# Stick-breaking norms for two pairs of heads at once, scaled later, with filling products from the first head on

## The chip, the cores and the metric

The kernel runs on one core of a Trainium2 chip. The metric is the device time of one execution in microseconds (us); lower is better. Five engines work side by side, each through a queue of its own in order: TensorE (PE, matrix products and transposes; its weight loads are shown apart as PEld), VectorE (DVE), ScalarE (ACT), GpSimd (POOL), and SyncE (SP), which issues the DMAs. They wait for each other by semaphores. Tiles live in SBUF, TensorE's results in the banks of PSUM.

## The reference

A residual stream of 512 tokens by 1024 passes two layers of FFN, hybrid mixer, cross attention and FFN, and then two layers of a second block. The change is about the stick-breaking heads of the mixer and what follows them. There are 8 heads of width 64. For each head, with z = q.k/8 and a strictly causal mask:

```
log_beta    = log_sigmoid(z)
log_1m_beta = where(causal, log_beta - z, 0)
between     = reverse_cumsum(log_1m_beta) - log_1m_beta
a           = where(causal, exp(log_beta + between), 0)
sb          = rms_norm(a @ v, sb_out_norm)        # per head, over its 64 values
h           = h + concat(sb, go) @ w_out          # go: gated-DeltaNet heads
h           = h + cross_attention(rms_norm(h), rms_norm(mem))
```

## The kernel before

Everything is float32, and a product of two float32 matrices is made as three products of rounded parts: each operand is split into a high part (`xh`, `wh`, `mh`, `gh`: a cast on ScalarE) and a low part (`xl`, `wl`, `ml`, `gl`: a subtraction on VectorE). Activations lie feature-major, 128 features by 512 tokens to a tile.

A mixer ends with the stick-breaking stage (`stick`, `heads_in_turn`). Heads run in turn, two to a *pair*, and head `hd` is one ahead of head `hd - 1`. For a head, TensorE makes the scores in three PSUM banks (`psz`, L989, L994), ScalarE two sigmoids of each (`sc`, `sb`; L1059, L1060), VectorE four running products along the keys (*scans*, L1064; 128, 384, 256 and 512 columns), and GpSimd multiplies both (L1065). Then ten transposes (L1011), in three groups of 4, 3 and 3 with a PSUM tile `pst` each, turn these weights; ScalarE, VectorE, ScalarE copy them (L1014). After an odd head, `pair_values` (L1028) multiplies the turned weights of both heads with the values into one bank, `pso`.

`use` then norms the pair: copy (`sacc`) and square (`ssq`) on ScalarE; sums over the 64 rows of each head by four small products (L1075); on VectorE mean and epsilon (`sbs`, L1078) and the reciprocal root as an integer start and three Newton steps, twelve instructions of 8 columns (`rsqrt`, L382 to L388, result `sbr`); on TensorE a broadcast of the factors (L1083); on VectorE the scaling (L1084) and the split into `mh`, `ml` (L394, L395).

To keep TensorE busy between these, `fills` deals out *filling products* in steps of six: first the mixer's output product of the other heads (`psd<-gh,wh` and so on, 512 columns, 16 steps), then the memory keys of the cross attention (`psd<-mem,wh`, 256 columns, 32 steps). `STICK_FILL` says how many steps go out after a head's scores, and at its transposes; what is left is drained at the end. The stage has PSUM banks for 2 fills (`d`), 3 scores (`z`), 2 of tag `t` (transposes, sums, broadcasts) and 1 of values.

The cross attention begins with two products that need no norm: the memory values (`x_v`, 16 steps of 12 products) and the rest of the mixer's output product, which reads `mh` and `ml` (`self.rest`, 16 steps). `XV_STEPS` deals them out in turn, 4 and 4.

The order on each engine is laid down when the program is built: the framework takes the instructions in the order of the code, with the weight loads, casts and subtractions (`wr`, `wh`, `wl`; L266 to L268) moved ahead by a priority, and places each by its own estimate of when it can start. On the chip every engine then takes its queue strictly in that order.

Of the kernel before, what the change touches and what calls it, by code (L numbers as in the profile page):

```python
# [18 lines left out]
P = 128  # L19
D = 1024  # L20
S = 512
# [13 lines left out]
AHEAD_FIRST = 70  # L35
ON_POOL = ()
PBUFS = (2, 2, 2, 2)
STICK_FILL = ((0,),) + ((1, 1, 2),) * 8
PARTS_AFTER = 8
PARTS_AHEAD = 1  # L40
XV_STEPS = (4, 4, 4, 0)
DIL_FILL = ((8,),) + ((4, 2, 2),) * 8
FOX_FILL = ((8,), (4, 2, 2), (1, 1, 1), (1, 1, 0), (0, 1, 1), (0, 1, 1), (0, 1, 1), (0, 1, 1), (0, 0, 1))

# [133 lines left out]
class Builder:  # L178
# [193 lines left out]
        return fill  # L372


    def rsqrt(self, x, out, tag):

        nc = self.nc
        n = x.shape[1]
        t = self.small([P, n], tag + "_t", 2)
        y = self.small([P, n], tag + "_y", 2)  # L380
        hx = self.small([P, n], tag + "_h", 2)
# [51 lines left out]
    def mean_rsqrt(self, m, out, eps=1e-6, n=D):  # L433

        self.nc.vector.tensor_scalar(out=m, in0=m, scalar1=1.0 / n, scalar2=eps, op0=ALU.mult, op1=ALU.add)
        self.rsqrt(m, out, "rs")

    def stats(self, h, width=S, tag="n"):

# [254 lines left out]
    def gdn_project(self, T, l, xh, xl, rc, R):  # L694
# [72 lines left out]

        rn = T([P, 2, H, NT], "rn")
        f3 = lambda x: x.rearrange("p a b c -> p (a b c)")
        self.rsqrt(f3(ss), f3(rn), "rq")  # L770
# [159 lines left out]
    def gdn_norm(self, T, t, state, o):  # L930

        nc = self.nc
        H = 4
        z = state["zt"][t]
        sq = self.xp.tile([P, H, P], F32, name=self.uid("osq"), tag="sq", bufs=1)
        nc.scalar.activation(out=sq, in_=o, func=AF.Square)
        so = self.small([P, H], "so")
        nc.vector.tensor_reduce(out=so, in_=sq, op=ALU.add, axis=AX.X)
        nc.vector.tensor_scalar(out=so, in0=so, scalar1=1.0 / GD, scalar2=1e-6, op0=ALU.mult, op1=ALU.add)
        ro = self.small([P, H], "ro")  # L940
        self.rsqrt(so, ro, "rp")
# [89 lines left out]
    def stick(self, T, l, qp, kp, v, mh, ml, fill):  # L1031
# [20 lines left out]
        def weights(hd):  # L1052
# [13 lines left out]
                    p[t] = bt  # L1066
            return p

        def use(pr, op):
            ot, sq = (self.xp.tile([P, S], F32, name=self.uid("s" + n), tag=n, bufs=1) for n in ("acc", "sq"))  # L1070
            nc.scalar.copy(ot, op)
            nc.scalar.activation(out=sq, in_=op, func=AF.Square)
            ssp = self.ps("t", [P, NT, 2])
            for t in range(NT):
                nc.tensor.matmul(ssp[:, t], sq[:, t * P : (t + 1) * P], self.c("pair"), start=True, stop=True)  # L1075
            f = lambda x: x.rearrange("p a b -> p (a b)")
            ss, ro = self.small([P, NT, 2], "sbs", 2), self.small([P, NT, 2], "sbr", 2)
            nc.vector.tensor_scalar(out=ss, in0=ssp, scalar1=1.0 / 64, scalar2=1e-6, op0=ALU.mult, op1=ALU.add)  # L1078
            self.rsqrt(f(ss), f(ro), "sbq")
            ps = self.ps("t")  # L1080
            for t in range(NT):
                for e in range(2):
                    nc.tensor.matmul(ps[64 * e : 64 * e + 64, t * P : (t + 1) * P], ro[:, t, e : e + 1].to_broadcast([P, 64]), self.c("ident"), start=True, stop=True)  # L1083
            nc.vector.scalar_tensor_tensor(out=ot, in0=ot, scalar=gn[:, pr : pr + 1], in1=ps, op0=ALU.mult, op1=ALU.mult)  # L1084
            self.split(mh[:, pr], ml[:, pr], ot)

        self.heads_in_turn(weights, v, T, use, fill)


    def memory_stats(self, T):  # L1090
# [39 lines left out]
    def xattn(self, h, l):  # L1130
        nc = self.nc
        H, W = XH, MEM
        with self.kvs, self.scope(self.uid("xa")) as xp, self.banks(d=3, n=1, z=2, t=2):
# [6 lines left out]
                self.split(v[0][:, t, c], v[1][:, t, c], ps, self.mem_c[:, t : t + 1])  # L1140

            steps = self.dense_tm_steps("x_v", l, 8, self.memp[:, 0], self.memp[:, 1], use_v, nt=2)
            for n in XV_STEPS:
                for _ in range(4):
                    next(self.rest)
                for _ in range(n):
                    next(steps)
            self.drain(self.rest)
            self.drain(steps)
            xh, xl, rc, R = self.norm(h, self.g("xattn_norm", l))  # L1150
# [65 lines left out]
    def final_and_norm(self, h, gain):  # L1216
# [24 lines left out]
        def factors():  # L1241
            m = self.small([P, 2, NT], "ms2", 1)
            ps = self.ps("n", [P, 2, NT])
            for i, x in enumerate((acc, acc2)):
                for j in range(NT):
                    nc.tensor.matmul(ps[:, i, j : j + 1], x[:, j * P : (j + 1) * P], self.c("one"), start=True, stop=True)
            nc.vector.tensor_scalar(out=m, in0=ps, scalar1=1.0 / D, scalar2=None, op0=ALU.mult)
            nc.vector.tensor_scalar(out=m[:, 0], in0=m[:, 0], scalar1=1e-6, scalar2=None, op0=ALU.add)
            nc.vector.scalar_tensor_tensor(out=m[:, 1], in0=m[:, 0], scalar=1e-6, in1=m[:, 1], op0=ALU.mult, op1=ALU.add)
            flat = lambda x: x.rearrange("p a b -> p (a b)")  # L1250
            self.rsqrt(flat(m), flat(both_r), "rs2")

        R = xt("R")
        self.pending.append(factors)
# [52 lines left out]
    def qk_project_steps(self, T, name, l, xh, xl, rc, fox):  # L1307
# [17 lines left out]
        self.rsqrt(flat(ss), flat(rr), "hq")  # L1325
# [80 lines left out]

    def heads_in_turn(self, weights, v, T, use, fill):

        p, pTs = {}, []
        for hd in range(9):  # L1410
            if hd < 8:
                p[hd] = weights(hd)
            if hd == 0:
                fill(0, 0)
                continue
            last = hd - 1
            pTs.append(self.turned_weights(p.pop(last), T, last % 2, fill=lambda i: fill(hd, i)))
            if last % 2:
                use(last // 2, self.pair_values(pTs, v, last // 2))
                pTs = []  # L1420
        fill(9, 0)

    def fox_decay(self, T, fa, l):

# [17 lines left out]
    def second(self, h, l, pT, after_final=False):  # L1442
        nc = self.nc
        self.turn_bank = "n"
        with self.scope(self.uid("sec")) as sp, ExitStack() as st:
# [37 lines left out]
            for _ in range(PARTS_AFTER):  # L1483
# [5 lines left out]
            self.turn_bank = 't'  # L1489
            dil = self.c("dil")  # L1490
            ob = half("ob")
            self.causal_attention(
                T,
                parts_b,
                v,
                None,
                lambda hd, t: dil[:, 384 - t * P : 512],
                lambda pr, ps: nc.vector.tensor_copy(ob[:, pr], ps),
                self.fills([("fq", qk("s_qa")), ("fv", values("s_va")), ("gb", gate("s_gb")), ("fk", qk("s_ka"))], DIL_FILL, got),
                ready,  # L1500
            )
# [154 lines left out]
```

## Time and profile before

| what | value |
|---|---|
| runs | 3204.21, 3196.81, 3198.81 us |
| median | 3198.81 us |
| profiled execution, its own time | 3195.22 us |
| its span, first to last instruction | 3192.9 us |
| TensorE's mean granted clock in it | 0.994 of 2.4 GHz |
| TensorE busy | 3134.1 us, 98% |
| VectorE busy | 2326.2 us, 73% |
| ScalarE busy | 1451.7 us, 45% |
| GpSimd busy | 133.8 us, 4% |

All rows are of the one profiled execution. The page gives sums over the whole span; a table by windows gives the same for stretches, with the granted clock (1.00 is 2.4 GHz, 0.50 is 1.2 GHz). A list of waits names the instruction that waited and the one that let it go. A timeline gives each instruction's start and length, with like neighbours merged into one row. Matmuls are pipelined: the spacing of their starts is what one costs, not the length in its row.

### The profile page before, as it was taken

The numbers are of one execution on the slowest core, as the hardware profiler recorded it, in microseconds if no ns is written. First come the engines' busy times: TensorE is split into PE (matmuls) and PEld (weight loads), VectorE is DVE, ScalarE is ACT, GpSimd is POOL, SyncE is SP. The second block draws the span as 40 slices with busy tenths as digits, with TensorE's granted clock in tenths as the row PEclk, the third lists the DMA queues.
The fourth block names the chain that finished last, engine by engine and source line by source line (L and its number), as shares of the span: only waits on it lengthen the run. The fifth ranks groups of instructions, "written<-read, shape, count | busy, mean of one in ns | idle before, by whom it ended". The sixth has DMA issues, their size and how long they took to land. (4 is left out here: it accounts for less than half of the span.)

```text
span 3192.9 us, 50423 instructions
## 1 busy us (share of the span) xinstructions
PE 3134.1 (98%) x20520; PEld 2718.9 (85%) x20520; DVE 2326.2 (73%) x3952; ACT 1451.7 (45%) x2291; POOL 133.8 (4%) x182
## 2 busy tenths in 40 slices
PE   8999999989999999999999989999999999999999
PEld 7999877778889998999877868889998987799877
DVE  8887567776588877888657686578886667766675
ACT  5344542544443434334452354453343556445563
POOL 0000002220000000000002040000000000000000
PEclk9999999999999999999999999999999999999999
DMA  4332220323233323333221223133332322223223
GB/s 165 97 118 81 87 73 28 95 71 113 67 125 95 107 76 117 100 103 101 70 86 34 82 65 119 60 125 99 101 95 72 100 80 80 76 90 100 72 73 101
DMA packets 86728, 287.32 MB, mean 90 GB/s; under 512 B 10080, under 2 KB 13408, under 8 KB 86496
## 3 DMA queue, kind: packets, MB, share of 16 engines
q1 hardware_dynamic: 86496, 284.10, 28.7%
q8 instruction: 161, 2.64, 0.3%
q14 instruction: 71, 0.58, 0.1%
HBM read 269.38 MB, written 2.10 MB: 85 GB/s over the span
## 5 line engine op out<-in xcount | busy, mean ns | idle before, releaser
L268 DVE TENSOR_TENSOR wl<-wr,wh 128x1024 fp32r<-128x1024 f32 (+3 forms) x384 | 443.1, 1154 | 211.4 <-ACT wh L267 209.4
L267 ACT CAST wh<-wr 128x1024 fp32r<-128x1024 f32 (+3 forms) x384 | 378.1, 985 | 399.4 <-PE psd L274 285.9
L394 ACT CAST sh<-sr 128x1024 fp32r<-128x1024 f32 x252 | 264.8, 1051 | 503.7 <-PE psd L580 474.4
L274 PE MATMUL psd<-xh,wh 128*128 128x512 f32 x960 | 387.0, 403 | 7.2 <-ACT xh L397 7.2
L274 PE MATMUL psd<-xl,wh 128*128 128x512 f32 x960 | 385.5, 402 | 0.2 <-DVE xl L398 0.2
L274 PE MATMUL psd<-xh,wl 128*128 128x512 f32 x960 | 384.9, 401 | 0.2 <-DVE wl L268 0.2
L580 PE MATMUL psd<-xh,sl 128*128 128x256 f32 x1152 | 322.7, 280 | 5.2 <-DVE sl L395 5.2
L580 PE MATMUL psd<-xh,sh 128*128 128x256 f32 x1152 | 322.5, 280 | 0.0
L580 PE MATMUL psd<-xl,sh 128*128 128x256 f32 x1152 | 321.9, 279 | 0.0
L395 DVE TENSOR_TENSOR sl<-sr,sh 128x1024 fp32r<-128x1024 f32 x252 | 307.3, 1220 | 15.1 <-ACT sh L394 14.2
L274 PE MATMUL psd<-wh,xh 128*128 128x256 f32 (+1 forms) x1024 | 292.1, 286 | 1.0 <-ACT wh L267 0.9
L274 PE MATMUL psd<-wh,xl 128*128 128x256 f32 (+1 forms) x1024 | 289.9, 283 | 1.2 <-DVE xl L398 1.1
L274 PE MATMUL psd<-wl,xh 128*128 128x256 f32 (+1 forms) x1024 | 289.0, 283 | 0.0
L274 PE MATMUL psd<-ah,wh 128*128 128x512 f32 x704 | 278.2, 395 | 0.0
L274 PE MATMUL psd<-al,wh 128*128 128x512 f32 x704 | 278.0, 395 | 0.0
L274 PE MATMUL psd<-ah,wl 128*128 128x512 f32 x704 | 277.0, 394 | 0.0
L274 PEld LDWEIGHTS psd<-xh,wh 128*128 128x128 f32 x960 | 181.2, 189 | 53.9 <-ACT xh L397 7.2
L580 PEld LDWEIGHTS psd<-xh,sl 128*128 128x128 f32 x1152 | 216.9, 188 | 6.8 <-DVE sl L395 6.8
L580 PEld LDWEIGHTS psd<-xh,sh 128*128 128x128 f32 x1152 | 216.8, 188 | 5.3
L580 PEld LDWEIGHTS psd<-xl,sh 128*128 128x128 f32 x1152 | 216.8, 188 | 4.8
L274 PEld LDWEIGHTS psd<-xh,wl 128*128 128x128 f32 x960 | 181.5, 189 | 42.1 <-issue 1.2
L274 PEld LDWEIGHTS psd<-xl,wh 128*128 128x128 f32 x960 | 181.5, 189 | 39.9 <-DVE xl L398 1.0
(452 smaller groups left out, 6999.2 us busy)
## 6 DMA issues: line engine op xcount, KB each, us to landing
sr<-w_ffn_in_dram SPq DMA_DIRECT2D x144, 512.0 KB, 3.9
wr<-w_ffn_out_dram SPq DMA_DIRECT2D x96, 384.0 KB, 4.0
wr<-w_ffn_in_dram SPq DMA_DIRECT2D x32, 512.0 KB, 3.8
wr<-w_mix_gdn_dram SPq DMA_DIRECT2D x24, 512.0 KB, 3.7
B<-B SPq DMA_DIRECT2D x40, 256.0 KB, 3.4
wr<-w_ffn_out_dram SPq DMA_DIRECT2D x16, 512.0 KB, 3.4
wr<-w_mix_qk_dram SPq DMA_DIRECT2D x16, 512.0 KB, 3.8
wr<-w_x_k_dram SPq DMA_DIRECT2D x16, 512.0 KB, 3.7
```

Source lines behind the costliest of these rows:

```text
L267: nc.scalar.copy(hi, raw)
L268: (nc.gpsimd if name in ON_POOL else nc.vector).tensor_sub(lo, raw, hi.bitcast(F32))
L274: mm = lambda a, b, first, last: nc.tensor.matmul(ps, a, b, start=first, stop=last, skip_group_check=flip)
L394: nc.scalar.copy(hi, src)
L395: nc.vector.tensor_tensor(out=lo, in0=src, in1=hi.bitcast(F32), op=ALU.subtract)
L580: nc.tensor.matmul(ps[:, j], w[a][:, k, fs], x[b][:, k], start=start and i == 0, stop=k == 3 and i == 2, skip_group_check=True)
```

## The change

Three things are changed, in both layers alike.

The norm of a pair is cut into functions. `use` makes the copy and the square at once as before (the copy of an even pair goes to tile `R`, of an odd pair to `acc`), and returns what is left as a list: for an even pair the sums alone; for an odd pair the sums with one reciprocal root for both pairs (16 columns), an empty step, the scaling of the even pair, and that of the odd pair. `heads_in_turn` takes one function of the list after each of a head's fills, but for the one in the middle. What the last pair leaves goes to the cross attention, which runs it between steps of the memory values.

`STICK_FILL` deals two steps after the first head's scores and five per head in place of four. `XV_STEPS` now holds, in turn, how many of the left-over functions, of the steps of the values and of the rest of the output product.

All norms of the kernel share one set of scratch tiles (`nr_t`, `nr_y`, `nr_h`) in place of a set for each caller.

```diff
-STICK_FILL = ((0,),) + ((1, 1, 2),) * 8
+STICK_FILL = ((2,),) + ((1, 2, 2),) * 8
-XV_STEPS = (4, 4, 4, 0)
+XV_STEPS = ((1, 4, 0), (3, 4, 12), (0, 4, 4))
...
-        t = self.small([P, n], tag + "_t", 2)
+        t = self.small([P, n], "nr_t", 3)
...
+        held = []
+
         def use(pr, op):
-            ot, sq = (self.xp.tile([P, S], F32, name=self.uid("s" + n), tag=n, bufs=1) for n in ("acc", "sq"))
+
+            ot, sq = (self.xp.tile([P, S], F32, name=self.uid("s" + n), tag=n, bufs=1) for n in (("R", "acc")[pr % 2], "sq"))
             nc.scalar.copy(ot, op)
             nc.scalar.activation(out=sq, in_=op, func=AF.Square)
...
+            if pr % 2 == 0:
+                held.append(self.small([P, 2, NT, 2], "sbs", 2))
+            ss = held[-1]
+
+            def sums():
+                ssp = self.ps("t", [P, NT, 2])
+                for t in range(NT):
+                    nc.tensor.matmul(ssp[:, t], sq[:, t * P : (t + 1) * P], self.c("pair"), start=True, stop=True)
+                nc.vector.tensor_scalar(out=ss[:, pr % 2], in0=ssp, scalar1=1.0 / 64, scalar2=1e-6, op0=ALU.mult, op1=ALU.add)
+
+            def scaled(pr, ot, ro):
+                ps = self.ps("t")
+                for t in range(NT):
+                    for e in range(2):
+                        nc.tensor.matmul(ps[64 * e : 64 * e + 64, t * P : (t + 1) * P], ro[:, pr % 2, t, e : e + 1].to_broadcast([P, 64]), self.c("ident"), start=True, stop=True)
+                nc.vector.scalar_tensor_tensor(out=ot, in0=ot, scalar=gn[:, pr : pr + 1], in1=ps, op0=ALU.mult, op1=ALU.mult)
+                self.split(mh[:, pr], ml[:, pr], ot)
+
+            if pr % 2 == 0:
+                held.append(ot)
+                held.append(ss)
+                return [sums]
+            ro = self.small([P, 2, NT, 2], "sbr", 2)
+            even = held[-2]
+
+            def factors():
+                sums()
+                flat = lambda x: x.rearrange("p c a b -> p (c a b)")
+                self.rsqrt(flat(ss), flat(ro))
+
+            return [factors, lambda: None, lambda: scaled(pr - 1, even, ro), lambda: scaled(pr, ot, ro)]
+
+        self.after = self.heads_in_turn(weights, v, T, use, fill)
...
-            for n in XV_STEPS:
-                for _ in range(4):
-                    next(self.rest)
+
+            for first, n, rest in XV_STEPS:
+                for _ in range(first):
+                    self.after.pop(0)()
                 for _ in range(n):
                     next(steps)
+                for _ in range(rest):
+                    next(self.rest)
...
-        p, pTs = {}, []
+
+
+        p, pTs, later = {}, [], []
+
+        def then(hd, i):
+            fill(hd, i)
+            if later and i != 1:
+                later.pop(0)()
+
...
-            pTs.append(self.turned_weights(p.pop(last), T, last % 2, fill=lambda i: fill(hd, i)))
+            pTs.append(self.turned_weights(p.pop(last), T, last % 2, fill=lambda i: then(hd, i)))
             if last % 2:
-                use(last // 2, self.pair_values(pTs, v, last // 2))
+                later = use(last // 2, self.pair_values(pTs, v, last // 2)) or []
```

How the orders differ is shown at three places of the first layer (the second layer's are alike). First VectorE's queue at the second pair's norm, before. `pst` is read for the sums, `sc` are the next head's scans, `sbr` the factors, `sacc` the pair being scaled.

```order
L1078 TENSOR_SCALAR sbs_6467<-pst_6462 128x8
L382 TENSOR_SCALAR sbq_t_6470<-sbs_6467 128x8
...
L1064 SCALAR_TENSOR_TENSOR sc_1064_6504<-sc_1064_6504,consts 128x128
L383 TENSOR_SCALAR sbq_y_6471<-sbq_t_6470 128x8
L1064 SCALAR_TENSOR_TENSOR sc_1064_6504<-sc_1064_6504,consts 128x384
...
L1064 SCALAR_TENSOR_TENSOR sc_1070_6526<-sc_1070_6526,consts 128x512
...
L388 SCALAR_TENSOR_TENSOR sbr_6468<-sbq_t_6470,sbq_y_6471 128x8
L268 TENSOR_TENSOR wl_6797<-wr_6795,wh_6796 128x1024
L1084 SCALAR_TENSOR_TENSOR sacc_6458<-sacc_6458,gains,pst_6485 128x512
```

And now, at the same pair, where one chain serves two pairs; `memT` frees a bank (`psd`) of the memory keys, `pT` is a copy of turned weights.

```order
L1064 SCALAR_TENSOR_TENSOR sc_1076_6542<-sc_1076_6542,consts 128x256
L1084 TENSOR_SCALAR sbs_6262<-pst_6563 128x8
L382 TENSOR_SCALAR nr_t_6569<-sbs_6262 128x16
...
L1064 SCALAR_TENSOR_TENSOR sc_1079_6552<-sc_1079_6552,consts 128x512
L386 TENSOR_TENSOR nr_t_6569<-nr_y_6570 128x16
L1014 COPY pT_1087_6592<-pst_6591 128x384
L387 TENSOR_TENSOR nr_t_6569<-nr_t_6569,nr_h_6571 128x16
L1146 TENSOR_TENSOR memT_6607<-psd_6395,mem_r 128x256
...
L268 TENSOR_TENSOR wl_6710<-wr_6708,wh_6709 128x1024
...
L388 SCALAR_TENSOR_TENSOR sbr_6522<-nr_t_6569,nr_y_6570 128x16
L1064 SCALAR_TENSOR_TENSOR sc_1099_6650<-sc_1099_6650,consts 128x128
```

The chain now has three scans of one head ahead of it, one scan, a copy, a bank's release, a weight's low part and a split inside, and the next head's scans behind it.

Second, TensorE's queue at the same place, before: sums (`ssq`), fills (24 in all, three rows of them shown), the broadcast of `sbr`, and the transposes of the head.

```order
L1075 MATMUL pst_6462<-consts,ssq_6459 128x2 x4
L989 MATMUL psz_6521<-mh_5970,ml_5971 128x512 x2
...
L274 MATMUL psd_6570<-mem_6536,wh_6572 128x256 x2
L274 MATMUL psd_6570<-mem_6536,wl_6573 128x256
L989 MATMUL psz_6620<-B_1030_6354,ml_5971 128x128
L1083 MATMUL pst_6485<-consts,sbr_6468 64x128 x8
L1011 MATMUL pst_6583<-consts,sb_1033_6368 128x128
```

And now (`psd_6612` is the bank that `memT` of the piece above frees).

```order
L1083 MATMUL pst_6563<-consts,ssq_6519 128x2 x4
L1011 MATMUL pst_6584<-consts,sb_1050_6426 128x128
...
L274 MATMUL psd_6611<-mem_6361,wl_6615 128x256
L1011 MATMUL pst_6625<-consts,sb_1050_6426 128x128
...
L274 MATMUL psd_6612<-mem_6361,wh_6614 128x256 x2
...
L989 MATMUL psz_6643<-B_1047_6412,ml_5971 128x128 x2
...
L1090 MATMUL pst_6683<-consts,sbr_6522 64x128 x8
L1011 MATMUL pst_6695<-consts,sb_1072_6529 128x128
```

Between the sums and the broadcast there now stand ten transposes, 24 fills, the next head's scores and 6 fills; before there were two score products, a mask and 24 fills.

Third, TensorE's queue at the end of the stage, before: the last pair's values, 10 fills, sums, 19 fills, the broadcast, and then the rest of the memory keys.

```order
L1028 MATMUL pso_6901<-pT_1152_6876,v_5480 64x128
...
L1075 MATMUL pst_6914<-consts,ssq_6911 128x2 x4
...
L1083 MATMUL pst_6937<-consts,sbr_6920 64x128 x8
...
L274 MATMUL psd_6950<-mem_6536,wl_6983 128x256
```

And now: 36 fills, the sums, 48 products of the memory values (`psd<-wh,mem`), and the broadcasts of two pairs.

```order
L274 MATMUL psd_6927<-mem_6361,wl_6974 128x256
L1083 MATMUL pst_7021<-consts,ssq_6956 128x2 x4
L274 MATMUL psd_7048<-wh_7043,mem_6361 128x256
...
L1090 MATMUL pst_7107<-consts,sbr_6959 64x128 x8
L1090 MATMUL pst_7119<-consts,sbr_6959 64x128 x8
```

The last two pairs are scaled in the cross attention's stage, behind the first four steps of the memory values; the output product that reads them stands 48 products later.

## Rows read from the trace of the kernel before

**Rows 1.** The page, engines: busy us (share of the span) xinstructions.

```profile
PE 3134.1 (98%) x20520; PEld 2718.9 (85%) x20520; DVE 2326.2 (73%) x3952; ACT 1451.7 (45%) x2291; POOL 133.8 (4%) x182
```

**Rows 2.** Windows: stretch and length, busy us of each engine, PEclk, DMA share, GB/s.

```profile
600.00:720.00 120.00, 105.16 (x701) 86.09 (x700) 90.41 (x157) 65.47 (x121) 35.25 (x32) 0.94 0.26 77
720.00:860.00 140.00, 139.96 (x763) 118.15 (x761) 86.76 (x139) 65.57 (x114) 0.00 (x0) 1.00 0.28 91
1820.00:1940.00 120.00, 104.84 (x689) 85.93 (x688) 89.43 (x154) 64.44 (x119) 35.24 (x32) 0.93 0.25 75
1940.00:2080.00 140.00, 139.97 (x763) 118.20 (x762) 86.20 (x139) 64.93 (x113) 0.00 (x0) 1.00 0.29 91
```

**Rows 3.** TensorE's waits, 605 to 715 us: us in total, times, longest.

```profile
PE pst L1083 <- DVE sbr L388: 10.4, 4, 3.5
PE pst L1011 <- POOL sb L1065: 2.3, 1, 2.3
PE pst L1011 <- DVE pT L1014: 1.2, 1, 1.2
PE psz L989 <- DMA mh<-mh: 0.8, 1, 0.8
```

**Rows 4.** TensorE's waits, 1825 to 1935 us.

```profile
PE pst L1011 <- DVE pT L1014: 1.4, 1, 1.4
```

**Rows 5.** Windows around single waits, columns as in rows 2.

```profile
619.00:625.00 6.00, 5.59 (x26) 4.43 (x27) 5.74 (x7) 2.96 (x6) 6.00 (x6) 0.72 0.00 0
...
670.00:676.00 6.00, 5.03 (x35) 4.17 (x35) 3.57 (x9) 1.98 (x4) 0.29 (x1) 0.72 0.27 87
...
1909.00:1919.00 10.00, 7.67 (x47) 7.10 (x47) 5.75 (x13) 2.22 (x5) 1.09 (x1) 0.66 0.16 54
...
1848.00:1851.00 3.00, 1.57 (x9) 1.31 (x9) 3.00 (x5) 2.58 (x5) 3.00 (x3) 1.00 0.50 130
```

**Rows 6.** TensorE's timeline, second pair: start, length, instruction, [idle before it <-releaser].

```profile
661.76 0.84 PE L989 MATMUL psz<-mh,ml 128*128 128x128 f32 x4
...
664.52 0.48 PE L274 MATMUL psd<-mem,wh 128*128 128x256 f32 x2
...
667.43 0.22 PE L989 MATMUL psz<-B,ml 128*128 128x128 f32 x1
670.97 1.38 PE L1083 MATMUL pst<-consts,sbr 128*64 128x128 f32 x16 [3.33 <-DVE sbr L388]
...
676.94 0.93 PE L1011 MATMUL pst<-consts,sb 128*128 128x128 f32 x7
```

**Rows 7.** VectorE's timeline, 653 to 681 us.

```profile
653.03 3.76 DVE L1064 TENSOR_TENSOR_SCAN sc<-sc,consts 128x128 f32<-128x128 f32 x4
656.71 0.53 DVE L1014 COPY pT<-pst 128x384 f32<-128x384 f32 x1
...
660.46 1.23 DVE L268 TENSOR_TENSOR wl<-wr,wh 128x1024 fp32r<-128x1024 f32 x1 [0.20 <-ACT wh L267]
...
664.10 0.17 DVE L1078 TENSOR_SCALAR sbs<-pst 128x8 f32<-128x8 f32 x1 [2.42 <-PE pst L1075]
...
669.33 0.99 DVE L388 SCALAR_TENSOR_TENSOR sbq_y<-sbq_t,sbq_y 128x8 f32<-128x8 f32 x1
...
670.75 0.17 DVE L388 SCALAR_TENSOR_TENSOR sbr<-sbq_t,sbq_y 128x8 f32<-128x8 f32 x1
...
680.42 0.41 DVE L1125 TENSOR_TENSOR memT<-psd,mem_r 128x256 f32<-128x256 f32 x1
```

**Rows 8.** GpSimd's timeline: the products of heads 4 and 5.

```profile
653.61 4.66 POOL L1065 TENSOR_TENSOR sb<-sb,sc 128x127 f32<-128x127 f32 x4 [9.95 <-DVE sc L1064]
...
669.21 1.09 POOL L1065 TENSOR_TENSOR sb<-sb,sc 128x511 f32<-128x511 f32 x1 [1.33 <-DVE sbq_t L386]
```

**Rows 9.** VectorE by shape: xcount, busy us, mean ns, idle before.

```profile
L388 DVE SCALAR_TENSOR_TENSOR sbr<-sbq_t,sbq_y 128x8 f32<-128x8 f32 x8 | 1.3, 166 | 0.3
L388 DVE SCALAR_TENSOR_TENSOR hrr<-hq_t,hq_y 128x32 f32<-128x32 f32 x8 | 1.5, 190 | 0.2
```

More of the change, by code (lines that the diff above doesn't have):

```diff
@@ L372, in fills, with rsqrt @@
         return fill
-    def rsqrt(self, x, out, tag):
+    def rsqrt(self, x, out):
         nc = self.nc
         n = x.shape[1]
-        t = self.small([P, n], tag + "_t", 2)
-        y = self.small([P, n], tag + "_y", 2)
-        hx = self.small([P, n], tag + "_h", 2)
+        t = self.small([P, n], "nr_t", 3)
+        y = self.small([P, n], "nr_y", 3)
+        hx = self.small([P, n], "nr_h", 3)
         nc.vector.tensor_single_scalar(t.bitcast(I32), x.bitcast(I32), 1, op=ALU.logical_shift_right)
@@ L435, in mean_rsqrt @@
         self.nc.vector.tensor_scalar(out=m, in0=m, scalar1=1.0 / n, scalar2=eps, op0=ALU.mult, op1=ALU.add)
-        self.rsqrt(m, out, "rs")
+        self.rsqrt(m, out)
     def stats(self, h, width=S, tag="n"):
@@ L769, in gdn_project @@
         f3 = lambda x: x.rearrange("p a b c -> p (a b c)")
-        self.rsqrt(f3(ss), f3(rn), "rq")
+        self.rsqrt(f3(ss), f3(rn))
         f, ir = T([P, NT, H], "xa"), T([P, H, NT], "ir")
@@ L940, in gdn_norm @@
         ro = self.small([P, H], "ro")
-        self.rsqrt(so, ro, "rp")
+        self.rsqrt(so, ro)
         nc.gpsimd.tensor_tensor(out=z, in0=o.rearrange("p h c -> p (h c)"), in1=z, op=ALU.mult)
@@ L1067, in weights @@
             return p
+        held = []
         def use(pr, op):
-            ot, sq = (self.xp.tile([P, S], F32, name=self.uid("s" + n), tag=n, bufs=1) for n in ("acc", "sq"))
+            ot, sq = (self.xp.tile([P, S], F32, name=self.uid("s" + n), tag=n, bufs=1) for n in (("R", "acc")[pr % 2], "sq"))
             nc.scalar.copy(ot, op)
             nc.scalar.activation(out=sq, in_=op, func=AF.Square)
-            ssp = self.ps("t", [P, NT, 2])
-            for t in range(NT):
-                nc.tensor.matmul(ssp[:, t], sq[:, t * P : (t + 1) * P], self.c("pair"), start=True, stop=True)
@@ L1076, in use @@
[L1076 to L1083, printed above, removed]
@@ L1084, in use @@
-            nc.vector.scalar_tensor_tensor(out=ot, in0=ot, scalar=gn[:, pr : pr + 1], in1=ps, op0=ALU.mult, op1=ALU.mult)
-            self.split(mh[:, pr], ml[:, pr], ot)
-        self.heads_in_turn(weights, v, T, use, fill)
+            if pr % 2 == 0:
[6 more added lines that the diff above has]
+                nc.vector.tensor_scalar(out=ss[:, pr % 2], in0=ssp, scalar1=1.0 / 64, scalar2=1e-6, op0=ALU.mult, op1=ALU.add)
@@ L1250, in factors @@
             flat = lambda x: x.rearrange("p a b -> p (a b)")
-            self.rsqrt(flat(m), flat(both_r), "rs2")
+            self.rsqrt(flat(m), flat(both_r))
         R = xt("R")
@@ L1324, in qk_project_steps @@
         rr = self.small([P, NT, 8], "hrr", 2)
-        self.rsqrt(flat(ss), flat(rr), "hq")
+        self.rsqrt(flat(ss), flat(rr))
         for t in range(NT):
@@ L1416, in heads_in_turn @@
             last = hd - 1
-            pTs.append(self.turned_weights(p.pop(last), T, last % 2, fill=lambda i: fill(hd, i)))
+            pTs.append(self.turned_weights(p.pop(last), T, last % 2, fill=lambda i: then(hd, i)))
             if last % 2:
-                use(last // 2, self.pair_values(pTs, v, last // 2))
+                later = use(last // 2, self.pair_values(pTs, v, last // 2)) or []
                 pTs = []
         fill(9, 0)
+        return later
     def fox_decay(self, T, fa, l):
@@ L1491, in second, with use_b @@
             ob = half("ob")
+            def use_b(pr, ps):
+                nc.vector.tensor_copy(ob[:, pr], ps)
             self.causal_attention(
@@ L1497, in second @@
                 lambda hd, t: dil[:, 384 - t * P : 512],
-                lambda pr, ps: nc.vector.tensor_copy(ob[:, pr], ps),
+                use_b,
                 self.fills([("fq", qk("s_qa")), ("fv", values("s_va")), ("gb", gate("s_gb")), ("fk", qk("s_ka"))], DIL_FILL, got),
```

## The prediction, written before the changed kernel was run

> **What bounds the kernel now.** I read the page's engine line first: TensorE (PE) is busy for 98% of the span and VectorE (DVE) for 73% [rows 1]. So only TensorE's missing 59 us, and any time at its lower clock, can be won without taking work away. The table by stage came next, with the stick-breaking stages (600 to 720 us and 1820 to 1940 us, one per layer) apart from the cross attention behind each. TensorE is busy for 105.2 and 104.8 of 120 us there, and for 140.0 of 140 us in both cross attentions [rows 2]. Half of all that TensorE misses lies in the two stages that the change touches.
>
> Then TensorE's waits in the two stages. Four waits in each are for `sbr`, the norm's factors that VectorE makes: 10.4 us in each layer, the longest 3.5 us. One is for GpSimd's product (2.3 us), one for VectorE's copy of transposed weights (1.2 and, in the second layer, 1.4 us) [rows 3, 4]; the rest of the second layer's list reads as the first's. Last, the granted clock just after such waits: it falls from 2.4 to 1.2 GHz, and a stretch of 6 us has a mean of 0.72, that is 0.28 x 6 = 1.7 us lost. Each layer has three long waits for `sbr`; five of the six such stretches have 0.72, the sixth, at 1909 us, has 0.66 over 10 us, 3.4 us lost. Two more with 0.72, one in each layer, follow the wait for GpSimd (619 us is the first). After the shorter wait of 1.4 us the clock stays at 1.00 [rows 5].
>
> Why `sbr` is late can be read in the first layer's second norm. TensorE finishes what it has at 667.4 + 0.2 us and waits until 670.97 [rows 6]. VectorE starts the norm at 664.10 and ends it at 670.75 + 0.17, 6.8 us, although its twelve small instructions take 0.17 us each when alone: the next head's four scans stand between them, and one of the twelve took 0.99 us [rows 7]. It ended with GpSimd's product (669.21 + 1.09 = 670.30; 669.33 + 0.99 = 670.32) [rows 7, 8].
>
> **The change, part by part.** *The waits for the factors.* The broadcasts of the factors (L1083 before, L1090 after) move from behind one group of fills to behind two heads' transposes, or, for the last two pairs, into the cross attention's stage. If the new places are covered, 2 x 10.4 = 20.8 us of waits go [rows 3], and 5 x 1.7 + 3.4 = 11.9 us of lost clock [rows 5]. The waits for the copy (1.2 + 1.4) go too: twelve 512-column fills now stand ahead of the third group of transposes. Gross: 35.3 us. The wait for GpSimd with its clock, and 0.8 us for a transfer at the stage's start, stay: nothing in front of them is moved.
>
> *The norm itself.* Two chains per layer in place of four, each 16 wide. An instruction of the chain takes 166 ns at 8 columns and 190 ns at 32 [rows 9], so 16 cost between these, and 24 instructions a layer (4 us at least) leave VectorE. TensorE gains from that only through the waits. Sharing one set of scratch tiles among all norms costs nothing: only VectorE writes and reads them, in order.
>
> *The moved fills.* One more step per head, so 36 products (256 columns) are left at the stage's end in place of 96. Their number is the same, so TensorE's work is unchanged; on their way they fill the place of the old waits. SP's weight loads change their order with them (output projection after four loads for the values). TensorE did not wait in that stage before [rows 2]; two staging tiles still run ahead. I take nothing; the other bound is one wait like today's, 3.5 us a layer.
>
> *Is VectorE in time for the new place?* I walk the first layer from the start of the scores of head 5, 661.76 in the trace; call it 0. TensorE: scores and sums 2.8 (661.76 to 664.52), ten transposes about 1.3 (seven took 0.9), 24 fills 2.9 (664.52 to 667.43) [rows 6]. At about 7.0 it wants the second bank of the memory keys, which VectorE frees with `memT` in the middle of the chain (the order shows it behind the fifth instruction of the norm). Then come 6 fills, scores and 6 fills, about 3.2, and the factors are wanted at 10.2 or later. VectorE: first scan at about 1.7 (an estimate: ScalarE has a copy, a square and a sigmoid of half a microsecond each ahead of it); three of the scans, held up by GpSimd, about half of the 3.8 us that four took in head 4 [rows 7]; sums and three small ones to 4.2; the fourth scan 1.3 to 5.5; a square and GpSimd's product behind it to 6.4; the copy 0.5 to 6.9; a multiply held by the last product (1.1) to 7.6; `memT` 0.4 to 8.0 [rows 7, 8]. So TensorE waits 1.0 us there. The rest of the chain with a weight's low part (1.2) and a split (about as long as `memT`) ends at about 10.8, while TensorE, delayed, comes at 11.2. **The old wait is gone, and a bank is late in its place.**
>
> The same walk gives three more in each layer: head 2's second transposes need a bank that VectorE frees (sums of pair 0) only behind head 3's scans, 0.6; the values of pair 2 wait for a copy behind a weight and a split, 0.4; head 6's second transposes come before the sums of pair 2 are read, 1.0. Together 3.0 us a layer, 6.0 in all. Each alone is bounded by nothing below and by one set of scans, 3.8 us, above [rows 7]. None is as long as 2.3 us, so the clock should hold as it did after 1.4 [rows 5].
>
> *The last two pairs.* Their chain stands behind 36 fills and the sums; 48 products of 256 columns follow, 5.8 us by twice the 24 [rows 6]. The chain takes 2 us alone and had 6.8 with four scans in it [rows 7], and no scans are left. Covered; without cover at most 1 us a layer. The output projection comes 48 products after the last scaling and reads the last pairs' parts last. I take nothing.
>
> **Sum.** The profiled execution took 3195.2 us, its span 3192.9 us and 2.3 us around it. 35.3 - 6.0 = 29.3 us come off: 3165.9 us. It lies 3.6 us under the median of the three runs, 3198.8 us; on that footing the forecast is 3169.5, rounded 3170.
>
> **Rivals.** *The new waits are long.* At the late bank and at head 6's transposes VectorE is 2 us later than I reckon in each layer, and the clock falls again: 4 x (2 + 1.7) = 14.8 us, so 3185. For it: VectorE was busy for 90 of 120 us [rows 2], and its heads with memory-key fills need about as long as TensorE's. Against: 4 us of chain a layer are gone, and TensorE now has 60 more fills in these heads.
>
> *No new wait at all:* 35.3 us come off, 3163.5. For it: banks may be freed earlier than an order with pauses lets me see.
>
> *VectorE and GpSimd cannot overlap.* If all their work in the stage excluded each other, its length would be 90.4 + 35.2 - 6.0 (two chains as they were: 6.8 less 3.8 for the scans, twice) = 119.6 us, as now [rows 2, 7]: TensorE's waits would only move, and the time would be 3198. For it: the 0.99 us above, and scans and products alternate in head 4 (3.8 us for both kinds) [rows 7, 8]. Against: VectorE's busy time already holds such stops, and a copy from PSUM took 0.53 us while a product ran [rows 7, 8]. The Trainium skill, "SBUF — State Buffer", section "Who interferes with whom", has this as a rule: a VectorE instruction with two SBUF inputs and a GpSimd instruction that reads SBUF exclude each other for the whole instruction. By that rule, the stopped multiply in the trace agrees, and the copy from PSUM is free.
>
> *Slower.* VectorE runs a whole set of scans late at the four places: a wait of 3.8 us with 1.7 of clock at each, 5.5 x 8 = 44 us against the 35.3 gained: 3198.8 + 8.7 = 3207.5. It decides from 3.5 us a wait on. For it: VectorE takes its queue in order, and at three of the places scans stand in front. Against: TensorE has 12 to 24 fills (1.4 to 2.9 us) between the scores that the scans need and these places.
>
> **How the numbers follow.** Forecast 0.61 (own range 3163 to 3177); long new waits 0.17 (3177 to 3190); no new wait 0.11; no overlap 0.06; slower 0.05. About 0.2%, 6.4 us, is what a measurement can tell from no change. The first three are faster: 0.89; the fourth is the same: 0.06; slower 0.05. The range goes from the no-wait case less 2 us of scatter, 3161, to the long waits, 3185.
>
> **What would show it.** Right: no wait of TensorE for `sbr` over 1 us; TensorE idle for about 6 us in each stick-breaking stage in place of 15, and each stage some 14 us shorter; the clock at 1.00 but for the two places behind GpSimd's wait; short waits for `memT` and `sbs`. Wrong: waits over 2 us at L1011 or at the memory-key products, with the clock at 0.5 behind them; or a new wait for `mh` or for a weight in the cross attention.

## The result, and the profile after

The kernel before ran in 3197.93 us (median of 4 runs, 3196.81 to 3204.21), the changed kernel in 3164.78 us (median of 4, 3162.87 to 3166.07). The ratio is 0.9898, 95% interval 0.9886 to 0.991: 33 us faster. The forecast was 3170 us, the range 3161 to 3185. The profiled execution took 3162.87 us; its span is 3160.9 us, 32.0 less than before.

The first line below is the page's line of engines, the others the table by windows (columns as in [rows 2]); the second stage now starts 16 us earlier.

```profile
PE 3120.6 (99%) x20520; PEld 2707.1 (86%) x20520; DVE 2316.1 (73%) x3904; ACT 1451.2 (46%) x2291; POOL 139.7 (4%) x182
...
600.00:720.00 120.00, 113.67 (x809) 95.50 (x809) 93.34 (x143) 72.67 (x132) 38.11 (x32) 0.99 0.33 99
720.00:860.00 140.00, 139.96 (x716) 116.03 (x715) 86.61 (x138) 62.43 (x110) 0.00 (x0) 1.00 0.26 83
1805.00:1925.00 120.00, 113.96 (x802) 95.16 (x801) 94.06 (x143) 72.29 (x130) 38.11 (x32) 0.99 0.32 95
1925.00:2065.00 140.00, 139.96 (x716) 116.12 (x715) 85.61 (x137) 63.10 (x110) 0.00 (x0) 1.00 0.26 83
```

TensorE misses 6.3 of 120 us in the first stage in place of 14.8 [rows 2], and the clock there is 0.99 in place of 0.94. The cross attention behind is as full as before, although it now holds the last two pairs' scaling. TensorE's waits in the first stage (605 to 715 us; columns as in [rows 3]):

```profile
PE pst L1011 <- POOL sb L1065: 2.3, 1, 2.3
PE pst L1011 <- DVE sR L1091: 1.3, 1, 1.3
PE psd L274 <- DVE memT L1146: 1.0, 1, 1.0
PE psz L989 <- DMA mh<-mh: 0.8, 1, 0.8
PE pst L1011 <- DVE sbs L1084: 0.5, 1, 0.5
PE psd L274 <- DVE h L646: 0.4, 1, 0.4
```

No wait for `sbr` is left of the four, 10.4 us, in [rows 3], and none for the copy `pT`. The second layer's list is the same without the last line. The two waits at the stage's second half on TensorE's timeline, first layer:

```profile
666.87 0.51 PE L274 MATMUL psd<-mem,wh 128*128 128x256 f32 x2 [0.96 <-DVE memT L1146]
...
670.15 1.09 PE L1090 MATMUL pst<-consts,sbr 128*64 128x128 f32 x16
671.18 0.66 PE L1011 MATMUL pst<-consts,sb 128*128 128x128 f32 x4
...
673.77 0.55 PE L1011 MATMUL pst<-consts,sb 128*128 128x128 f32 x3 [1.34 <-DVE sR L1091]
```

The broadcast at 670.15 waits for nothing: its factors were ready. But it fills a bank of tag `t`, and the head's second group of transposes needs that bank. VectorE empties it with the scaling of `sR`, which on its own timeline stands behind the next head's four scans:

```profile
669.20 0.17 DVE L388 SCALAR_TENSOR_TENSOR sbr<-nr_t,nr_y 128x16 f32<-128x16 f32 x1
669.30 3.77 DVE L1064 TENSOR_TENSOR_SCAN sc<-sc,consts 128x128 f32<-128x128 f32 x4
673.00 0.72 DVE L1091 SCALAR_TENSOR_TENSOR sR<-sR,gains,pst 128x512 f32<-128x512 f32 x1
```

The clock (seventh figure of a line): the stretch behind the wait for GpSimd, and the one behind the wait for `sR`.

```profile
619.00:625.00 6.00, 5.60 (x24) 4.50 (x25) 6.00 (x7) 3.29 (x6) 6.00 (x6) 0.72 0.00 0
...
673.00:679.00 6.00, 5.23 (x49) 4.36 (x51) 5.78 (x10) 3.03 (x6) 1.55 (x2) 1.00 0.27 87
```

Of eight stretches at the lower level in the two stages, two are left, one a layer, behind the wait for GpSimd.

**Where the time came from.** TensorE starts the same 20,520 products and transposes in both kernels, and outside the stages in the same order, so the two traces can be laid over each other by number. From the 4,200th to the 5,200th, which encloses the first stage, the changed kernel is 14.2 us shorter (174.1 to 159.9); from the 12,120th to the 13,100th, which encloses the second, 16.1 us (171.3 to 155.2). Together 30.3 us of the 32.0. The rest is outside: 0.9 and 0.7 us of a shorter wait for weights (`sl`) at the start of two FFNs, which no run ties to the change. Between the 6,208th and the 8,200th, inside FFNs, both take 313.75 us.

### The profile page after: what moved, and what is told of

Its sections match the earlier page's. It is cut to its first block, busy times and chain, and to the rows that moved or that the text cites. A ratio compares the mean times of both kernels' runs of the same rounds, so it can differ in the third digit from the quotient of the medians.

```text
span 3160.9 us, 50355 instructions
## 1 busy us (share of the span) xinstructions
PE 3120.6 (99%) x20520; PEld 2707.1 (86%) x20520; DVE 2316.1 (73%) x3904; ACT 1451.2 (46%) x2291; POOL 139.7 (4%) x182
## 5 line engine op out<-in xcount | busy, mean ns | idle before, releaser
L395 DVE TENSOR_TENSOR sl<-sr,sh 128x1024 fp32r<-128x1024 f32 x252 | 307.4, 1220 | 15.0 <-ACT sh L394 14.2
```

The lines of the kernel that those rows point to most:

```text
L395: nc.vector.tensor_tensor(out=lo, in0=src, in1=hi.bitcast(F32), op=ALU.subtract)
```

## The experiments

Times are medians beside the kernel before on the same chip (3195.8 to 3198.0 us). "Stages" is the change against before, both stages together, measured between the numbered products as above. The times also hold what lies outside the stages, and that differs between executions of one kernel: one stretch at the lower clock, which one execution has there and another has not, was worth 1.5 us (last section).

| run | time, us | ratio to before (95%) | stages, us |
|---|---|---|---|
| e1 fills alone | 3193.7 | 0.9991 (0.9982 to 0.9999) | -0.8 |
| e2 norms alone | 3174.2 | 0.9923 (0.9911 to 0.9936) | -24.2 |
| e3 late, a root a pair | 3172.3 | 0.992 (0.9907 to 0.9932) | -30.5 |
| e4 two at once, not late | 3169.2 | 0.9913 (0.9899 to 0.9926) | -25.5 |
| e5 changed kernel again | 3164.6 | 0.9899 (0.9884 to 0.9914) | -30.4 |
| e6 as e3, same tiles | 3162.4 | 0.9897 (0.9881 to 0.9914) | -30.3 |
| e7 changed, one tile more | 3170.5 | 0.9919 (0.9904 to 0.9934) | -30.5 |
| e8 scaled together | 3163.5 | 0.9895 (0.9881 to 0.991) | -31.7 |
| e9 four steps first | 3166.2 | 0.9907 (0.9894 to 0.9921) | -29.8 |
| e10 six steps first | 3163.5 | 0.9898 (0.9885 to 0.9912) | -33.2 |
| e11 fills spread | 3173.6 | 0.9924 (0.991 to 0.9937) | -25.9 |
| e12 one scan less | 3163.6 | 0.9894 (0.9877 to 0.991) | -34.9 |

### The parts of the change

e1, the fills in the kernel before; e2, the changed kernel with the old fills:

```diff
# e1, in the kernel before
-STICK_FILL = ((0,),) + ((1, 1, 2),) * 8
+STICK_FILL = ((2,),) + ((1, 2, 2),) * 8
# e2, in the changed kernel: the same two lines the other way round
```

> The kernel before with the new count of filling steps alone (two after the first head, five per head); the norms are made and scaled at once, pair by pair, as before. Theory (the late scaling takes the waits away, the fills only cover its new places): TensorE still waits for the factors sbr four times a layer, about 9 us in place of 10.4, with most of the six lost stretches of clock still there; only the waits for the copy of transposed weights go. 3192 us (3188 to 3196). Rival (the extra fills are what covers the waits): sbr waits under 4 us a layer and at least half of the clock back, 3180 us or less.

> The changed kernel with the old count of filling steps (none after the first head, four per head), so the new norms alone. Theory (the parts need each other): no wait for sbr over 1 us, but 60 products of 256 columns a layer (7 us) lie at the stage's end again and not between the heads, so TensorE waits for scans, GpSimd products and copies about 4 to 6 us a layer more than in the changed kernel, one or two of these waits over 2 us with a dip of the clock behind: 3180 us (3174 to 3186). Rival (the norms alone are the change): 3164 to 3168 us, waits as in the changed kernel.

e1 took 3193.7 us, as the theory had it. TensorE's waits on its timeline in the first layer:

```profile
652.80 1.98 PE L1083 MATMUL pst<-consts,sbr 128*64 128x128 f32 x16 [3.55 <-DVE sbr L388]
...
675.95 0.78 PE L274 MATMUL psd<-mem,wh 128*128 128x256 f32 x2 [1.92 <-DVE memT L1125]
...
698.78 1.09 PE L1083 MATMUL pst<-consts,sbr 128*64 128x128 f32 x16 [3.34 <-DVE sbr L388]
...
716.66 1.09 PE L1083 MATMUL pst<-consts,sbr 128*64 128x128 f32 x16 [0.84 <-DVE sbr L388]
```

The long waits stand at the first and the third pair; at the second, the wait for `memT` takes the place of the one for `sbr`. Fills alone give nothing that the stages show. e2 came out between theory and rival, at the theory's lower edge: the waits for `sbr` are gone, but `sR` takes 2.9 us (1.3 in the changed kernel) with a dip of the clock behind it (0.72 from 669 to 675 us), and the copy `pT` 1.5 again. The fills are worth 6 us of stages with the new norms and 1 without.

e4 keeps the one root for two pairs but makes and scales it at once; e3 keeps the lateness with a root for each pair:

```diff
# e4, in the changed kernel
-XV_STEPS = ((1, 4, 0), (3, 4, 12), (0, 4, 4))
+XV_STEPS = ((0, 4, 0), (0, 4, 12), (0, 4, 4))
...
-                return [sums]
+                sums()
+                return []
...
-            return [factors, lambda: None, lambda: scaled(pr - 1, even, ro), lambda: scaled(pr, ot, ro)]
+            factors()
+            scaled(pr - 1, even, ro)
+            scaled(pr, ot, ro)
+            return []
# e3, in the changed kernel
+                r0 = self.small([P, 2, NT, 2], "sbr0", 2)
...
+                    self.rsqrt(flat(ss[:, 0]), flat(r0[:, 0]))
...
-                self.rsqrt(flat(ss), flat(ro))
+                self.rsqrt(flat(ss[:, 1]), flat(ro[:, 1]))
```

> The changed kernel with one root for two pairs as in it, but made and scaled at once behind the odd pair, not a head later; fills as in the changed kernel. Theory (lateness does it): two waits for sbr a layer are left, behind pairs 1 and 3, of about 3.5 and 2.5 us, each with a dip of the clock of 1.7 us, and the short waits for banks mostly go: 2 x (6 + 3.4) - 4 = about 15 us over the changed kernel, 3180 us (3173 to 3186). Rival (halving the number of chains does it): 3170 us or less.

> The changed kernel with a reciprocal root for each pair (four chains of 8 columns a layer in place of two of 16), each scaled at the same late place; TensorE's order is the same. Theory (lateness does it, the halved number of chains only spares VectorE time that nothing waits for): within 3 us of the changed kernel, 3166 us (3163 to 3169), the waits of TensorE the same but for up to 1 us a layer. Rival (two at once does it): VectorE has 4 us more a layer and is late at the banks behind it: waits of 2 us or more at the transposes of heads 3 to 7 and the clock falls behind them, 3174 us or more.

e4's time spoke for the rival, and e3's lay between the two (3172.3 us, where the theory ended at 3169 and the rival began at 3174). e4 took 3169.2 us where 3180 was expected. Its waits in the first layer:

```profile
668.12 0.51 PE L274 MATMUL psd<-mem,wh 128*128 128x256 f32 x2 [1.91 <-DVE memT L1150]
...
671.07 1.97 PE L1090 MATMUL pst<-consts,sbr 128*64 128x128 f32 x32 [1.04 <-DVE sbr L388]
...
703.50 1.97 PE L1090 MATMUL pst<-consts,sbr 128*64 128x128 f32 x32 [1.12 <-DVE sbr L388]
```

Making two norms at once removes the first and third pair's broadcasts, which are the two places where e1 waits 3.5 and 3.3 us. What is left is 1.0 and 1.1 us. So the theory that lateness is needed fell: pairing without it gives 25.5 of the 30.3 us.

e3 was 8 us over the changed kernel, yet its stages were as short (-30.5). The excess lay in the FFNs, whose products had not been touched: the 6,208th to the 8,200th took 314.97 us, not 313.75. The one thing that e3 adds and that reaches that far is its scratch tile `sbr0`. e6 is e3 without it (both halves of one `sbr`), e7 the changed kernel with it:

```diff
# e6, against e3
-                r0 = self.small([P, 2, NT, 2], "sbr0", 2)
...
+                held.append(self.small([P, 2, NT, 2], "sbr", 2))
...
# e7, against the changed kernel
-            ro = self.small([P, 2, NT, 2], "sbr", 2)
+            ro = self.small([P, 2, NT, 2], "sbr" if pr == 3 else "sbr0", 2)
```

> The changed kernel itself, as the control beside the three others of this set. Both theories below take it as their base: 0.99 of the kernel before, 3163 to 3166 us.

> A reciprocal root for each pair, scaled late, as in the earlier run, but without the scratch tile which that kernel had more than the changed one. Theory (the extra time of the earlier run came from its added tile, which moved other tiles, and not from the norms): within 2 us of the changed kernel, and the products of the FFNs as far apart as in it. Rival (two norms at once matter by themselves): 6 to 9 us over the changed kernel, as in the earlier run.

> The changed kernel, in the same order on every engine, with one more scratch tile of 64 bytes per partition in two buffers, so that tiles behind it lie elsewhere. Theory (place of the tiles): the products of the FFNs start 0.3 to 0.5% farther apart (187.2 us in place of 186.2 us for the same 1300 products), and the time is 6 to 9 us over the changed kernel. Rival (the unpaired norms made the difference): within 2 us of the changed kernel.

All three came out as the theory of the tile had it, to a few tenths of a microsecond: e6 lies 2.2 us under e5, and e7 5.9 us over it, with 314.95 us for the FFN products in place of e5's 313.80. The order of instructions is the same in e7 as in e5 on every engine. The table by windows in an FFN, for the changed kernel, and then for e7:

```profile
960.00:1160.00 200.00, 200.00 (x1394) 186.13 (x1393) 162.82 (x190) 79.53 (x97) 0.00 (x0) 1.00 0.32 101
```

```profile
960.00:1160.00 200.00, 200.00 (x1386) 186.17 (x1386) 163.09 (x190) 79.37 (x96) 0.00 (x0) 1.00 0.30 100
```

In both TensorE is never idle and the clock is 1.00, but e7 gets through 1386 products where the changed kernel does 1394. And e6, without the tile, shows what the pairing is worth when the scaling is late: nothing (3162.4 us, -30.3 in the stages; the same waits within 0.1 us in its first stage, but for `h`).

### What bounds the stage now

e8 moves the sums and both scalings behind the third group of transposes, away from the banks that waited:

```diff
-                return [sums]
+                return [lambda: None, sums]
...
-            return [factors, lambda: None, lambda: scaled(pr - 1, even, ro), lambda: scaled(pr, ot, ro)]
+            both = lambda: (scaled(pr - 1, even, ro), scaled(pr, ot, ro))
+            return [factors, lambda: None, lambda: None, both]
```

> The changed kernel with the sums of an even pair and both scalings moved behind the third group of transposes of a head, so that no bank of tag t waits for VectorE behind a head's scans. Theory (the waits for sbs and sR are banks freed behind the scans): 0.5 + 1.3 us a layer go, 3.7 us in all, to 3160 to 3162 us, with memT's wait of 1.0 as it was. Rival (VectorE is simply late, and what it is late with is only renamed): another wait of 1 to 2 us a layer at the next transposes or fills, the time within 1 us of the changed kernel.

The time says no gain (3163.5 against 3164.6 us on that chip), and the stages are 1.3 us shorter where 3.7 was expected. The waits that e8 has in its first stage and that stand in the place of `sR` and `sbs`:

```profile
PE psd L274 <- DVE h L646: 1.3, 2, 0.9
PE pst L1011 <- DVE pT L1014: 1.1, 1, 1.1
PE psd L274 <- DVE memT L1147: 1.0, 1, 1.0
```

`sR` and `sbs` are gone from the list and `pT` and a longer `h` are there: the rival was right. e9, e10 and e11 deal the filling steps out differently:

```diff
-STICK_FILL = ((2,),) + ((1, 2, 2),) * 8
# e9
+STICK_FILL = ((4,),) + ((1, 2, 2),) * 8
# e10
+STICK_FILL = ((6,),) + ((1, 2, 2),) * 8
# e11
+STICK_FILL = ((4,), (1, 2, 2), (1, 2, 2), (2, 2, 2), (1, 2, 2), (1, 2, 2), (3, 2, 2), (1, 2, 2), (1, 2, 2))
```

> The changed kernel with four filling steps after the first head's scores in place of two (12 products of 256 columns fewer at the stage's end). In TensorE's order seven more products of 512 columns (7 x 0.234 = 1.6 us) stand ahead of the first head's transposes. Theory (the products of GpSimd are done at a fixed time, so fills ahead of them shorten the wait): the wait for GpSimd falls from 2.35 to 0.7 us, the clock no longer falls behind it, 2 x 1.6 + 3.4 = about 5 us under the changed kernel, 0.988 of the kernel before, 3159 us. Rival (the wait is only moved on: the stage is as long as VectorE's and GpSimd's work in it): the waits further on grow by as much as this one shrinks, within 1.5 us of the changed kernel but for the clock.

> The changed kernel with six filling steps after the first head's scores (24 products of 256 columns fewer at the stage's end); 31 products of 512 columns stand between the first head's scores and its transposes in place of 8. Theory (fixed time of GpSimd): no wait for GpSimd and no dip of the clock behind it, 2 x 2.35 + 3.4 = about 8 us under the changed kernel, 3157 us. Rival (VectorE bounds the stage): from head 3 on only 256-column steps are left, 12 products a head in place of 18, each worth half the time: the waits for sbs, memT and sR grow by 2 to 4 us a layer and give it back, 3162 to 3167 us.

> As the one with four filling steps first, and one more step after head 3's scores and two more after head 6's, so that 6 products of 256 columns are left at the stage's end in place of 36. Theory (TensorE comes too early at the banks that VectorE frees behind a head's scans, and fills ahead of them cost nothing): the waits for sbs and sR (0.5 + 1.3 us a layer) go or fall under 0.3 us, 3 us under the kernel with four steps first, 3156 us. Rival (VectorE bounds the stage): the time stays within 1 us of that kernel, with waits at the stage's end or at other banks.

e9 shortens the wait for GpSimd to 1.6 us only, and `sR` and `pT` grow to 2.3 and 1.2; the stages gain nothing (-29.8), as its rival had it. In e10 the wait for GpSimd is gone; the whole list of its first stage is:

```profile
PE pst L1011 <- DVE sR L1091: 2.7, 1, 2.7
PE psz L989 <- DVE ml L395: 1.7, 1, 1.7
PE psd L274 <- DVE h L646: 1.3, 1, 1.3
PE pst L1090 <- DVE sbr L388: 0.4, 1, 0.4
```

6.1 us in place of 6.3: the same sum under other names. Its stages are 2.9 us shorter than the changed kernel's, but a median of 3163.5 us does not show it. The fall of the clock behind GpSimd's wait, which e10 no longer has, and which the expectations of e9, e10 and e12 count as a gain, is no part of that: e3 has no such fall in either stage, and its stages are as long as the changed kernel's (-30.5). The last section shows why.

e11 was the worst of them, against both expectations. Its stages are 4.4 us longer than the changed kernel's. Another 6.3 us of its profiled execution lie outside the stages, with three more stretches at the lower clock (at 1285, 2435 and 2862 us), and are not explained by the edit. In its first stage, VectorE, ScalarE and then TensorE, a fence each:

```profile
672.24 3.77 DVE L1064 TENSOR_TENSOR_SCAN sc<-sc,consts 128x128 f32<-128x128 f32 x4
675.93 0.39 DVE L1146 TENSOR_TENSOR memT<-psd,mem_r 128x256 f32<-128x256 f32 x1
```

```profile
676.36 0.41 ACT L394 CAST kT<-memT 128x256 fp32r<-128x256 f32 x1 [1.21 <-DVE memT L1146]
676.67 0.58 ACT L1014 COPY pT<-pst 128x512 f32<-128x512 f32 x1
```

```profile
677.30 0.86 PE L1011 MATMUL pst<-consts,sb 128*128 128x128 f32 x3 [2.60 <-ACT pT L1014]
```

The further memory-key products ahead of the transposes put a `memT` behind the scans; its cast on ScalarE waits for it, and the copy of the transposes stands behind that cast: a wait of 2.6 us, with a dip of the clock behind it (0.72 from 677 to 683 us).

e12 takes work from VectorE instead. It leaves out the third scan of each head:

```diff
+                    if t != 1:
-                    nc.vector.tensor_tensor_scan(out=ct[:, ::-1], ...
+                        nc.vector.tensor_tensor_scan(out=ct[:, ::-1], ...
```

> The changed kernel without the third of VectorE's four scans of each head (256 columns, 0.7 us; left out, so the weights of that part are not the reference's); TensorE's order is the same. Theory (VectorE's work between the heads sets the waits that are left): each wait that stands behind a set of scans shrinks by about 0.7 us: sR 1.3 to 0.6, sbs 0.5 to 0, memT 1.0 to 0.3 and GpSimd 2.35 to 1.6, together 2.6 us a layer, 5 us in all and up to 3.4 of clock: 3158 us (3155 to 3161). Rival (the waits are set by TensorE's order or by GpSimd, which has its products as before): the same waits within 0.3 us and 3164 us.

The stages fell by 4.6 us more, and the span with them (3158.4 us), but the median of 3163.6 does not show it. Each wait shrank by 0.2 to 0.4 us (GpSimd 2.0, `sR` 1.0, `memT` 0.8, `sbs` 0.2), half of the 0.7 expected. VectorE and then GpSimd at the same head as above:

```profile
667.88 1.27 DVE L1065 TENSOR_TENSOR_SCAN sc<-sc,consts 128x128 f32<-128x128 f32 x2
669.40 1.85 DVE L1065 TENSOR_TENSOR_SCAN sc<-sc,consts 128x512 f32<-128x512 f32 x1 [0.26 <-ACT sc L1059]
671.18 0.72 DVE L1092 SCALAR_TENSOR_TENSOR sR<-sR,gains,pst 128x512 f32<-128x512 f32 x1
```

```profile
668.47 4.27 POOL L1066 TENSOR_TENSOR sb<-sb,sc 128x127 f32<-128x127 f32 x4 [3.45 <-ACT sb L1060]
```

From the first scan to the scaling it is 3.3 us in place of 3.7. The scan that is gone had taken 0.8 us. Of that, 0.26 us now go into a wait of the last scan for ScalarE's sigmoid, and the last scan itself, 1.85 us, is no faster than it was. Here it is at the same head in the changed kernel, and then the last scan of the head before in e12, where GpSimd has paused:

```profile
671.25 1.82 DVE L1064 TENSOR_TENSOR_SCAN sc<-sc,consts 128x512 f32<-128x512 f32 x1
```

```profile
662.54 1.21 DVE L1065 TENSOR_TENSOR_SCAN sc<-sc,consts 128x512 f32<-128x512 f32 x1
```

The same 512 columns take 1.21 us while GpSimd pauses and 1.82 or 1.85 us while its products run. So the waits that are left are set by VectorE's scans at least in part, and these scans take longer beside GpSimd's products. GpSimd's share of the waits is not shown: no run took work from GpSimd alone. The Trainium skill has the exclusion in "SBUF — State Buffer", section "Who interferes with whom" (two SBUF inputs on VectorE and a GpSimd read exclude each other); the trace agrees with it here, 1.82 us against 1.21.

None of the versions is faster than the changed kernel by more than the runs scatter.

## Why the prediction was right, point by point

*Gross gain, 35.3 us.* All of it came: no wait for `sbr`, none of 0.2 us or more for `pT`, and the six stretches behind `sbr` at 0.72 and 0.66 are gone. The waits for GpSimd and for the transfer stayed to a tenth of a microsecond. The waits that went, less the new ones, make up 17.3 of the stages' 30.3 us; the 13.0 that are left are near the 11.9 reckoned for the clock. The prediction put no gain on the moved fills themselves, which e1 bears out, and let them cover the new places: e2 shows 6 us of stages for that.

*New waits, 6.0 us.* They sum to 6.1 us (3.2 in the first layer, 2.9 in the second). Two of the four named places hit: `memT` inside the chain, 1.0 predicted and 0.96 and 0.98 measured; `sbs` behind head 3's scans, 0.6 and 0.53, 0.54. Two did not come: pair 2's values (0.4) and head 6's transposes before the sums (1.0). In their place stands one that the walk overlooked, 1.34 us in each layer, and 0.4 for `h` in one. The walk asked when the factors are ready for the broadcast, and not when the bank that the broadcast fills becomes free. The 3.0 us a layer thus came out right by luck: 1.4 us of it did not come, and a wait that nobody had reckoned with made up for it.

*The clock.* "None is as long as 2.3 us, so the clock should hold": it held behind 1.34 us. The runs do not bear out 2.3 us as a bound, though (last section).

*The norm itself and the moved fills.* Costed at nothing. e6 bears out the first; of the second, no wait in the cross attention shows a price. The shared scratch tiles were not tried alone. *The last two pairs* are covered: TensorE has 139.96 of 140 us behind each stage.

*The sum.* 3165.9 us was forecast for the profiled execution and 3162.87 came. Of the 3.0 us, 1.0 lie in the stages, 1.6 in the starts of two FFNs, and 0.3 around the span (2.0 us in place of 2.3). The step from the profiled execution to the median added 3.6 us, and this execution lies 1.9 under its median; that is the other 1.7.

*The rivals.* Long new waits: no. Exclusion of VectorE and GpSimd: not as a whole, since the stages did shrink, but e8 to e12 point to VectorE for most of the waits that remain, with scans that take longer beside GpSimd's products. Slower: no; it took 3.5 us at each place, and the longest new wait is 1.34.

*What the prediction did not see* is that either half of the edit would do. It treated "two at once" as a saving of VectorE time worth nothing and lateness as the cause. With the new fills in place, each alone brings most of the gain (e4 25.5 us, e6 30.3 us of stages).

## What to carry to other kernels

A result that is moved to a later place in a queue also holds its bank from there: walk through when the bank is needed next and what stands in front of the instruction that empties it, not only through when the operand is ready. When several waits in a stage shift from name to name under every edit while their sum stays, look for the engine, or the pair of engines, that is behind all of them, and take work from it (e12 shortened the stages by 4.6 us that way, though its median does not show it). And lay two traces over each other by product number before naming a cause: a difference outside the stage that was edited can have a cause of its own, here a tile or a fall of the clock.

## What the runs showed of the hardware that was not expected

*One more tile changes the pace of TensorE.* One more scratch tile (64 bytes per partition, two buffers), with the same order on every engine, made FFN products 0.4% slower, 314.95 in place of 313.80 us for the same 1992 products with TensorE never idle, and the whole kernel about 6 us slower (e7 against e5 on the same chip; e3 the same). Since the order is the same, the likely cause is that the tiles behind it lie elsewhere, but this is not shown: no run records or varies the addresses.

*How long a wait is does not settle whether the clock falls.* The wait of 2.35 us for GpSimd was followed by the lower level in both layers of the changed kernel, but in e5, the same kernel again, and in e6 in the first layer only, and in e3 in neither. The table by windows for the second layer of the changed kernel, and then for that of e6, whose wait is 2.34 us:

```profile
1822.00:1828.00 6.00, 5.37 (x21) 4.04 (x22) 6.00 (x8) 2.67 (x5) 6.00 (x6) 0.72 0.00 1
...
1828.00:1840.00 12.00, 12.00 (x62) 9.53 (x61) 11.81 (x14) 8.36 (x16) 5.13 (x5) 1.00 0.31 89
```

```profile
1822.00:1828.00 6.00, 5.34 (x27) 3.74 (x28) 6.00 (x8) 4.12 (x7) 6.00 (x6) 1.00 0.00 1
...
1828.00:1840.00 12.00, 11.02 (x56) 8.50 (x55) 11.81 (x14) 6.91 (x13) 5.18 (x5) 1.00 0.31 89
```

Nor did the clock fall in e10's first layer, behind the wait of 2.7 us for `sR`:

```profile
668.00:676.00 8.00, 4.92 (x49) 4.36 (x47) 7.71 (x14) 5.37 (x11) 4.65 (x4) 1.00 0.19 66
```

In e10's second stage it fell behind a wait of 1.9 us, for a transfer (0.72 from 1816 to 1822 us). So the prediction's bound, "none as long as 2.3 us", held here but is no rule.

*What a fall costs depends on what TensorE meets next.* Each such fall takes 1.7 us of clock (0.28 x 6). But in the windows above TensorE then works through all of the next 12 us in the changed kernel, and is idle for 1.0 of them in e6, 0.9 us in a wait for `h` that VectorE ends. From the 12,120th to the 13,100th product both take 155.2 us: behind GpSimd's wait a fall costs the stage nothing. Elsewhere one did cost nearly all that it took. Between the 18,000th and the 19,000th product e5 has a fall, at 2790 us, that the first run of the same kernel has not, and takes 1.5 us longer. So two executions of one kernel can differ by a few microseconds with the same waits.
